# Splitting the second-to-last store of a streaming cross-entropy kernel by rows

## The chip, the cores and the metric

One NeuronCore of one Trainium2 chip runs the kernel. The metric is the device time of one execution in microseconds (us). A run's time is somewhat longer than the span that the profile shows, which goes from the first to the last instruction.

## The reference

Element by element, over two matrices of 8192 x 8192 float32:

```python
eps = 1e-7
pred = np.clip(pred, eps, 1 - eps)
return -(target * np.log(pred) + (1 - target) * np.log(1 - pred))
```

`target` holds only 0 and 1. So each element is -log(pred) or -log(1 - pred), and the kernel computes it as -Ln(|pred + target - 1|).

## The kernel before, in words

The matrices are taken as flat arrays of 128 x 524288 elements, cut into 40 chunks. A chunk of width w covers 128*w consecutive elements in memory, and tile row (partition) p holds the p-th run of w elements, so that a store of a chunk writes one contiguous block of memory, one run for each tile row. `plan` (line 17) lays them out: two of 5120 columns, 35 of 14336, and three at the end of 5632, 5632 and 1024. The last three have the numbers n-3, n-2 and n-1 and are called a, b and c. A tile row of chunk b is 22528 bytes, one of chunk c is 4096 bytes. `pred` and the result share one ring, `ring_p`, of three slots and a tail; `target` is cast to bf16 as it is loaded, into `ring_t`.

For each chunk, or each half of it, the steps are:

- `clip` (line 88, VectorE): max and min with eps.
- `log` (lines 94, 97, 98): VectorE adds target - 1, ScalarE takes the absolute value and then Ln, all in place.
- `back` (line 102, VectorE): times -1.
- `store`, to the output.

The order is written out by hand. Loads and most stores are issued from GpSimd (lines 72, 75, 79). The stores of a, b and c are issued from SyncE: `store` picks its queue by `k >= n - 3` (line 78) and issues one transfer of 128 rows (line 79), and `store_rows` (line 81) issues chunk c as three transfers, of rows 0-107, 108-119 and 120-127 (line 84). SyncE issues only these five transfers, in the order a, b, c, and each waits for the `back` of its chunk. After the last, at line 184, the program waits for all stores.

The end of the program is:

```python
        log(b, (1, 2))
        back(a, (1, 2))
        store(a)
        log(c)
        back(b, (0, 2))
        back(b, (1, 2))
        store(b)
        back(c)
        store_rows(c)
```

A DMA transfer is carried out by up to 16 DMA engines, which every queue of the core shares. In the trace each tile row of these stores is one packet on one DMA engine, and each engine that takes part in a transfer closes its share with a packet of 4 bytes.

Of the kernel before, what the change touches and what calls it, by code (L numbers as in the profile page):

```python
# [1 line left out]

# [4 lines left out]

EPS = 1e-7

BIG = 14 * 1024  # L10
FIRST = 5 * 1024
LAST = 5632
TAIL = 1024
SLOTS = 3


def plan(total):
    n = (total - 2 * FIRST - 2 * LAST - TAIL) // BIG
    assert n > 4 and total == 2 * FIRST + n * BIG + 2 * LAST + TAIL
    spots = [(FIRST, 0, 0), (FIRST, FIRST, FIRST)]  # L20
    spots += [(BIG, k % SLOTS * BIG, 0) for k in range(1, n + 1)]
    end = (n + 1) % SLOTS * BIG
    spots += [(LAST, end, 0), (LAST, end + LAST, LAST)]
    return spots + [(TAIL, SLOTS * BIG, BIG)]


@with_exitstack
def kernel(
    ctx: ExitStack,
    tc: tile.TileContext,  # L30
    pred: bass.AP,
    target: bass.AP,
    out: bass.AP,
):
    nc = tc.nc
    fp32 = mybir.dt.float32
    bf16 = mybir.dt.bfloat16
    Alu = mybir.AluOpType
    Act = mybir.ActivationFunctionType
    P = nc.NUM_PARTITIONS  # L40

    R, C = pred.shape
    spots = plan(R * C // P)
    n = len(spots)
    widths = [s[0] for s in spots]
    cols = [sum(widths[:k]) for k in range(n)]

    def chunk(ap, k):
        flat = ap.rearrange("r c -> (r c)")
        return flat[cols[k] * P : (cols[k] + widths[k]) * P].rearrange("(p w) -> p w", p=P)  # L50

    pool = ctx.enter_context(tc.tile_pool(name="rings", bufs=1))
    ring_p = pool.tile([P, SLOTS * BIG + TAIL], fp32, name="ring_p", tag="ring_p")
    ring_t = pool.tile([P, BIG + TAIL], bf16, name="ring_t", tag="ring_t")
    warm = pool.tile([1, 8], fp32, name="warm", tag="warm")

    def spot(k, part=(0, 1)):
        w, c, _ = spots[k]
        i, m = part
        return ring_p[:, c + i * w // m : c + (i + 1) * w // m]  # L60

    def spot_t(k, part=(0, 1)):
        w, _, c = spots[k]
        i, m = part
        return ring_t[:, c + i * w // m : c + (i + 1) * w // m]

    def load_p(k):
        if k == 0:
            for rows in (slice(0, P, 2), slice(1, P, 2)):
                nc.scalar.dma_start(out=spot(0)[rows], in_=chunk(pred, 0)[rows])  # L70
        else:
            nc.gpsimd.dma_start(out=spot(k), in_=chunk(pred, k))  # L72

    def load_t(k):
        nc.gpsimd.dma_start(out=spot_t(k), in_=chunk(target, k))  # L75

    def store(k):
        queue = nc.sync if k >= n - 3 else nc.gpsimd
        queue.dma_start(out=chunk(out, k), in_=spot(k))  # L79

    def store_rows(k):
        src, dst = spot(k), chunk(out, k)
        for first, last in ((0, 108), (108, 120), (120, 128)):
            nc.sync.dma_start(out=dst[first:last], in_=src[first:last])

    def clip(k, *part):
        p = spot(k, *part)
        nc.vector.tensor_scalar(  # L88
            out=p, in0=p, scalar1=EPS, scalar2=1 - EPS, op0=Alu.max, op1=Alu.min
        )  # L90

    def log(k, *part):
        p = spot(k, *part)
        nc.vector.scalar_tensor_tensor(  # L94
            out=p, in0=spot_t(k, *part), scalar=1.0, in1=p, op0=Alu.subtract, op1=Alu.add
        )
        nc.scalar.activation(out=p, in_=p, func=Act.Abs)  # L97
        nc.scalar.activation(out=p, in_=p, func=Act.Ln)  # L98

    def back(k, *part):  # L100
        p = spot(k, *part)
        nc.vector.tensor_scalar(out=p, in0=p, scalar1=-1.0, scalar2=None, op0=Alu.mult)  # L102

    with tc.manual_schedule():
        nc.vector.memset(warm, 1.0)  # L105
        load_t(0)
        load_p(0)
        load_t(1)
        load_p(1)
        load_p(2)  # L110
        nc.scalar.activation(out=warm, in_=warm, func=Act.Ln)  # L111
        for k in (0, 1):
            clip(k)
            log(k)
        load_t(2)
        back(0)
        store(0)
        back(1)
        store(1)
        load_p(3)  # L120
        a, b, c = range(n - 3, n)
        for k in range(2, n - 3):
            for h in (0, 1):
                clip(k, (h, 2))
                log(k, (h, 2))
            if k < n - 4:
                load_t(k + 1)
            else:
                load_t(a)
                load_t(b)  # L130
                load_p(c)
                load_t(c)
                back(k, (0, 2))
                for j in (a, b):
                    clip(j)
            if k < n - 4:
                back(k, (0, 2))
            back(k, (1, 2))
            store(k)
            if k + 2 < n - 3:  # L140
                load_p(k + 2)
            elif k + 2 == n - 3:
                load_p(a)
                load_p(b)
        log(a, (0, 2))
        log(a, (1, 2))
        clip(c)
        log(b, (0, 2))
        back(a, (0, 2))
# [3 lines that stand above are left out]
        log(c)  # L153
        back(b, (0, 2))
        back(b, (1, 2))
        store(b)
        back(c)
        store_rows(c)


# [1 line left out]
_INS = ['pred', 'target']  # L162
_OUTS = [((8192, 8192), 'float32')]


# [23 lines left out]
```

## Time and profile before

| | |
|---|---|
| time, median of 3 runs | 1865.05 us (1864.38 to 1865.44) |
| span of the profiled execution | 1863.3 us (the page gives no time of its own beside it) |
| VectorE busy | 1121.6 us, 60% |
| ScalarE busy | 902.4 us, 48% |
| GpSimd busy | 178.7 us, 10% |
| read from and written to memory | 536.87 MB and 268.44 MB, 432 GB/s over the span |
| SyncE's queue (q1) | 448 packets, 6.29 MB, 0.8% of the 16 DMA engines' span |
| stores a and b | 2816 KB each, 14.6 us from issue to landing (median) |
| store c | 432, 48 and 32 KB |

The median lies 1.75 us above the span of the profiled execution. The busy shares of engines are over the whole span; the change touches only the end of it, so the stretches of the last microseconds say more than the shares. In the stretches, "DMA share" is the mean busy share of the 16 DMA engines, so that 0.06 is about one engine.

### The profile page before, as it was taken

Reading aid. Unit: us, or ns where it says so; the run is one execution under the profiler, and the core shown is the slowest. Engines: PE = TensorE matmul, PEld = TensorE weight load, DVE = VectorE, ACT = ScalarE, POOL = GpSimd, SP = SyncE. Lnnn points to the kernel's source line nnn. Section 1 sums busy time; section 2 is a strip of 40 time slices with the busy share of each in tenths; the row PEclk is TensorE's granted clock in tenths of the full one; section 3 lists DMA queues with packets and bytes.
Section 4 is the critical chain, followed back from the end, with each engine's and each line's share of the span. In section 5 each row is a group of like instructions: output and inputs, shape, how many; then the busy total and the mean of one; then the engine's idle time right before and its main releaser. Section 6 shows DMA issues by size and latency. Waiting matters only on the chain.

```text
span 1863.3 us, 713 instructions
## 1 busy us (share of the span) xinstructions
DVE 1121.6 (60%) x230; ACT 902.4 (48%) x156; POOL 178.7 (10%) x120
## 2 busy tenths in 40 slices
DVE  4666555555666566655555666566655555666565
ACT  4454444455555544444445555544444445555554
POOL 1111101111110011101111110011101111110020
DMA  9999999999999999999999999999999999999999
GB/s 344 348 370 356 355 356 355 355 355 355 357 375 374 374 372 355 355 355 355 355 355 355 359 374 374 375 375 361 355 355 356 356 356 355 356 367 374 374 353 352
DMA packets 17318, 671.15 MB, mean 360 GB/s; under 512 B 1952, under 2 KB 1952, under 8 KB 2336
## 3 DMA queue, kind: packets, MB, share of 16 engines
q0 software_dynamic: 16704, 662.18, 99.0%
q1 hardware_dynamic: 448, 6.29, 0.8%
q10 hardware_dynamic: 160, 2.62, 0.4%
q14 instruction: 6, 0.05, 0.0%
HBM read 536.87 MB, written 268.44 MB: 432 GB/s over the span
## 4 chain that ended last, share of the span: by engine, by line
DMA 60%; issue 35%; ACT 3%; DVE 1%; POOL 0%; POOLq 0%; DVEq 0%; PEldq 0%
DMA ring_t<-in_target_dram 58%; DMA ring_p<-in_pred_dram 2%; ACT ring_p L98 1%; ACT ring_p L97 1%; DVE ring_p L94 1%; DVE ring_p L102 0%; POOL out_dram L79 0%; DVE ring_p L88 0%; POOL ring_t L75 0%; POOLq L75 0%; POOL ring_p L72 0%; POOLq L79 0%; DVEq L94 0%; PEldq L184 0%
## 5 line engine op out<-in xcount | busy, mean ns | idle before, releaser
L97 ACT ACTIVATE ring_p<-ring_p 128x7168 f32<-128x7168 f32 (+3 forms) x77 | 452.0, 5870 | 940.7 <-DVE ring_p L94 940.7
L94 DVE SCALAR_TENSOR_TENSOR ring_p<-ring_t,ring_p 128x7168 f32<-128x7168 bf16 (+3 forms) x77 | 558.2, 7251 | 372.0 <-DMA ring_t<-in_target_dram 370.7
L102 DVE TENSOR_SCALAR ring_p<-ring_p 128x7168 f32<-128x7168 f32 (+3 forms) x77 | 285.4, 3707 | 329.4 <-ACT ring_p L98 329.4
L98 ACT ACTIVATE ring_p<-ring_p 128x7168 f32<-128x7168 f32 (+3 forms) x77 | 452.6, 5877 | 2.4
L88 DVE TENSOR_SCALAR ring_p<-ring_p 128x7168 f32<-128x7168 f32 (+3 forms) x75 | 284.6, 3794 | 24.4 <-DMA ring_p<-in_pred_dram 24.4
L79 POOL DMA_DIRECT2D out_dram<-ring_p x37 | 128.0, 3459 | 584.4 <-DVE ring_p L102 584.2
L75 POOL DMA_DIRECT2D ring_t<-in_target_dram x40 | 29.0, 724 | 1057.2 <-DVE ring_p L94 1056.4
L72 POOL DMA_DIRECT2D ring_p<-in_pred_dram x39 | 21.8, 561 | 2.5 <-issue 2.5
L111 ACT ACT_TABLE_LOAD x1 | 1.3, 1283 | 1.9 <-issue 1.9
L105 DVE MEMSET warm<- 1x8 f32 x1 | 0.1, 65 | 0.8 <-PEq L173 0.8
L111 ACT ACTIVATE warm<-warm 1x8 f32<-1x8 f32 x1 | 0.2, 208 | 0.0
L173 POOL MEMSET const-float32-0.0<- 128x1 f32 x1 | 0.1, 99 | 0.2 <-issue 0.2
L173 POOL MEMSET const-bfloat16-1.0<- 128x1 bf16 x1 | 0.1, 102 | 0.0
L173 POOL MEMSET const-uint8-127<- 128x1 uint8 x1 | 0.1, 100 | 0.0
L173 POOL MEMSET const-float32-1.0<- 128x1 f32 x1 | 0.1, 99 | 0.0
## 6 DMA issues: line engine op xcount, KB each, us to landing
ring_p<-in_pred_dram POOLq DMA_DIRECT2D x35, 7168.0 KB, 44.3
out_dram<-ring_p POOLq DMA_DIRECT2D x35, 7168.0 KB, 31.1
ring_t<-in_target_dram POOLq DMA_DIRECT2D x35, 3584.0 KB, 31.3
ring_p<-in_pred_dram POOLq DMA_DIRECT2D x2, 2816.0 KB, 37.1
out_dram<-ring_p SPq DMA_DIRECT2D x2, 2816.0 KB, 14.6
out_dram<-ring_p POOLq DMA_DIRECT2D x2, 2560.0 KB, 27.9
ring_t<-in_target_dram POOLq DMA_DIRECT2D x2, 1408.0 KB, 26.5
ring_p<-in_pred_dram ACTq DMA_DIRECT2D x2, 1280.0 KB, 10.5
```

The source lines that it names most:

```text
L72: nc.gpsimd.dma_start(out=spot(k), in_=chunk(pred, k))
L75: nc.gpsimd.dma_start(out=spot_t(k), in_=chunk(target, k))
L79: queue.dma_start(out=chunk(out, k), in_=spot(k))
L88: nc.vector.tensor_scalar(out=p, in0=p, scalar1=EPS, scalar2=1 - EPS, op0=Alu.max, op1=Alu.min)
L94: nc.vector.scalar_tensor_tensor(out=p, in0=spot_t(k, *part), scalar=1.0, in1=p, op0=Alu.subtract, op1=Alu.add)
L97: nc.scalar.activation(out=p, in_=p, func=Act.Abs)
L98: nc.scalar.activation(out=p, in_=p, func=Act.Ln)
L102: nc.vector.tensor_scalar(out=p, in0=p, scalar1=-1.0, scalar2=None, op0=Alu.mult)
L105: nc.vector.memset(warm, 1.0)
L111: nc.scalar.activation(out=warm, in_=warm, func=Act.Ln)
L173: nc = _bacc.Bacc("TRN2", target_bir_lowering=False, num_devices=1)
```

## The change

Chunk b is stored by `store_rows` in place of `store`: three transfers on SyncE, of rows 0-111, 112-123 and 124-127, in place of one of 128 rows. They read and write the same bytes. `store_rows` now takes its cuts as arguments; chunk c keeps its own (108 and 120). The queue, the wait and the place in the order remain.

```diff
-    def store_rows(k):
+    def store_rows(k, *cuts):
         src, dst = spot(k), chunk(out, k)
-        for first, last in ((0, 108), (108, 120), (120, 128)):
+        for first, last in zip((0,) + cuts, cuts + (P,)):
             nc.sync.dma_start(out=dst[first:last], in_=src[first:last])
...
         back(b, (0, 2))
         back(b, (1, 2))
-        store(b)
+        store_rows(b, 112, 124)
         back(c)
-        store_rows(c)
+        store_rows(c, 108, 120)
```

## The prediction

> **What bounds the kernel now.** I read the page first, for what is busy over the whole span; then SyncE's waits and the DMA issues, for what the last wait is; then the stretches of the last 9 us; and at the end the trace's records of single DMA packets.
>
> The page:
>
> ```profile
> span 1863.3 us, 713 instructions
> DVE 1121.6 (60%) x230; ACT 902.4 (48%) x156; POOL 178.7 (10%) x120
> DMA  9999999999999999999999999999999999999999
> q1 hardware_dynamic: 448, 6.29, 0.8%
> ```
>
> No compute engine is busy for more than 60%, and the 16 DMA engines are busy in every slice: the kernel is bound by DMA. The change moves bytes between DMA engines in the last 16 us only, so that stretch decides. q1 is SyncE's queue.
>
> SyncE's waits and the timeline of its issues:
>
> ```profile
> SPq L184 <- DMA out_dram<-ring_p: 12.4, 3, 6.6
> ...
> 1847.07 0.35 SPq L79 DMA_DIRECT2D out_dram<-ring_p  x1
> ...
> 1847.45 0.69 DVE L102 TENSOR_SCALAR ring_p<-ring_p 128x1024 f32<-128x1024 f32 x1 [0.41 <-ACT ring_p L98]
> 1848.17 1.31 SPq L84 DMA_DIRECT2D out_dram<-ring_p  x3
> ```
>
> The last arithmetic ends at 1848.14, SyncE's last issue at 1849.48, and after that the program only waits for stores (L184, three waits, 12.4 us). So about 14 us of pure store draining stand at the end, and it is the slowest DMA engine that ends the span.
>
> The stretches (columns: window, its length, busy time of DVE, ACT and POOL, clock, DMA share, GB/s):
>
> ```profile
> 1857.00:1858.00 1.00, 0.00 (x0) 0.00 (x0) 0.00 (x0) 1.00 0.92 395
> 1859.50:1860.00 0.50, 0.00 (x0) 0.00 (x0) 0.00 (x0) 1.00 0.73 299
> 1860.00:1860.50 0.50, 0.00 (x0) 0.00 (x0) 0.00 (x0) 1.00 0.33 135
> 1860.50:1861.00 0.50, 0.00 (x0) 0.00 (x0) 0.00 (x0) 1.00 0.10 41
> 1861.00:1861.50 0.50, 0.00 (x0) 0.00 (x0) 0.00 (x0) 1.00 0.12 49
> 1861.50:1862.00 0.50, 0.00 (x0) 0.00 (x0) 0.00 (x0) 1.00 0.04 16
> ```
>
> All engines work up to about 1859.5, then they run out one by one over 2.4 us. That ragged edge is all that a different split of rows can win; what it can lose is not bounded so.
>
> **Who is late.** The packet records of q1 are 448 = 384 rows (256 of 22528 bytes for stores a and b, 128 of 4096 for c) and 64 marks of 4 bytes, one for each transfer and engine. A packet starts where the one before it on its engine ended, so they can be chained into 16 engines. Eight chains end with 9 + 1 + 1 rows of c and three marks, four with 9 + 1 rows and two marks, four have no row of c. So 108 rows went as 9 on each of 12 engines, 12 rows as one on each of 12, 8 rows as one on each of 8, and 128 rows as 8 on each of 16. I call the eight 0-7, the four 8-11, the four without c 12-15. By the same pattern (as many engines up to 16 as divide the count) 112 rows are 7 on each of 16, 12 rows one on each of 0-11, 4 rows one on each of 0-3.
>
> The ends of these chains, in span time: seven of 0-7 at 1859.67 to 1860.52; the eighth, which entered store b about a microsecond behind the rest, at 1861.44; three of 8-11 at 1859.83 to 1860.30; the fourth at 1861.97; 12-15, late since the POOL store ahead, at 1860.65 to 1860.99. The fourth of 8-11 is last because of its first two rows of c: they took 0.311 and 1.385 us where 123 of 128 took 0.159. Without that it would have ended at about 1860.6. From 1861.97 it is 1.3 us to the end of the span (landing, the remaining waits, closing barrier).
>
> **The change part by part.** (1) *Bytes.* 255 of 256 rows of 22528 took 0.836 us and the next starts 0.833 after; the total is unchanged. Engines 12-15 lose one row each: 1860.65 to 1860.99 becomes 1859.82 to 1860.16. This gains nothing by itself, since two other engines end after them. Engines 4-11 keep 8 rows of b and get one more mark (0.006 us). Engines 0-3 get nine rows and two more marks: +0.845.
>
> (2) *Issues.* Two more transfers on SyncE. The issues took 0.354 to 0.483 us, so two cost 0.75 to 0.95 on SyncE. Behind them stand the three issues of c; they move from 1848.17 to about 1848.4-1848.5, since SyncE waited there for the last L102 anyhow, and end near 1849.9. The first packet of c starts on its engine at 1857.95 because b is queued in front: over 7 us of cover, so the cost is zero. Without that cover it would be about 0.4. The 112 rows are issued at the same time as before, and nothing starts later: b's first row runs no earlier than 1851.3, when a's eight rows are through on the first engine. No compute engine waits on these stores.
>
> (3) *The closing waits.* Two more completions are waited for. Waits already fulfilled are 0.05 to 0.07 us apart, and b's come ahead of c's, so they pass while c still drains: 0 to 0.1 us, taken as zero.
>
> (4) *What the other split does to the rate of a row.* In the 128-row form every row ran at 0.836, with 16 engines at once. The trace has no 22528-byte row in any other split. The nearest is c: nearly all of its rows ran at 0.159 although the late engines were still in b, but three lost time (0.15, 1.23 and 0.58 us). From below the cost is nil (a row cannot go faster than its engine); from above it is in the rival. I take 0.2 us, nearer to c's common row than to its stalls, as a stall counts only on the engine that ends last.
>
> The sum, on the span: if the late eighth engine is one of 4-7, the end is 1861.45 without a stall like the one seen (-0.5) and 1861.97 with it (0); if it is one of 0-3, it is 1861.44 + 0.845 = 1862.28 (+0.3). The two halves even out near zero (+0.3 and about -0.3); with the 0.2 of part 4 that is +0.2. The page gives no time of the profiled execution but its span, 1863.3; the median of the runs, 1865.05, lies 1.75 above, which I carry over: 1863.3 + 0.2 + 1.75 = 1865.2.
>
> **The rivals.** *Crowding, slower.* The 12-row piece gives engines 0-11 neighbouring rows of the tile, and the 4-row piece gives 0-3 the last four. If four neighbouring rows can be read only at one engine's rate, each of these rows takes 4 x 0.836 = 3.34 us. Engines 0-3 do so twice: 6.69 in place of 0.84, +5.85, and their ends of 1859.67 to 1860.52 go to 1865.5 to 1866.4, which is 3.6 to 4.4 beyond 1861.97: 1868.6 to 1869.5. It decides once sharing adds more than 0.6 to 1.5 us in all to an engine of 0-3 (1861.97 less 1860.52 or 1859.67, less 0.845); below that the other engines cover it. For it: c's row at 0.311, twice 0.156, and the one at 1.385, both while other engines were in b. Against it: c's own 12 and 8 rows are such pieces, and four engines ran there in one 0.4 us stretch, each packet 0.159, while engines 12-15 kept 0.836 on every row. But c's rows are short, and engines were spread by their starts. A milder form (two engines meeting for part of a row) gives +1 to +3: 1866 to 1868.
>
> [...]
>
> *The split is not as said.* If 4 rows go to a single engine, it has 12 rows of b, +3.3 us on an engine that ended by 1860.52: at most 1863.9, so 1866.2 to 1867.0. Against it: 8 and 12 rows did spread over 8 and 12 engines.
>
> *The edge closes.* The stall does not recur and the late engine is among 4-11: 1864.5. The most that any split could win is the mean of the 16 ends, 1860.4: 1863.5. So faster by over 0.2% (3.7 us, about what a measurement of this kernel can tell from no change) has no room in this edge.
>
> **How the numbers follow.** The balance as summed, with or without the stall: 0.68, of it 0.15 for the edge that closes (1864.5). Crowding in full 0.12, in its milder form 0.14, another split 0.04; 0.02 for something the trace does not show. The forecast alone spans 1864.3 to 1866.3. The range reaches through the milder crowding to the lower end of the full one, 1864.2 to 1868.6, and leaves out most of the full one and a little below. Slower by over 0.2% is above 1868.8: most of the full crowding and what is unknown, 0.13. Faster 0.02, the rest 0.85.
>
> **What would show it.** Right: q1 with 464 records (384 rows and 64 - 16 + 32 = 80 marks), nearly all rows of b at 0.836, engines 12-15 finished before 1860.3, the last DMA share ending between 1861.3 and 1862.5, and three issues at 1847.1 to 1848.4 ahead of c's. Wrong: rows of 22528 at 1.6 to 3.4 us in the pieces of 12 and 4, and a DMA share of 0.2 to 0.3 that lasts beyond 1863 (crowding); or a single engine at work for 3 us (split).

## The result, and the profile after

The change makes the kernel slower: 1870.36 us (median of 7 runs, 1869.55 to 1870.70) against 1864.44 us (7 runs, 1864.25 to 1865.44) on the same chip. The ratio is 1.0030, with a 95% interval of 1.0019 to 1.0040. The forecast was 1865.2, its range ended at 1868.6, and slower by over 0.2% had a chance of 0.13. The profiled run took 1870.42 us with a span of 1868.6, so that 1.8 us lie around the span, as before.

The page of the kernel after:

```profile
span 1868.6 us, 715 instructions
DVE 1121.6 (60%) x230; ACT 902.4 (48%) x156; POOL 178.6 (10%) x120
q1 hardware_dynamic: 464, 6.29, 0.9%
```

SyncE's waits (total, times, longest):

```profile
SPq L184 <- DMA out_dram<-ring_p: 16.9, 1, 16.9
```

Arithmetic and bytes are what they were, and the 464 packets are those that were foreseen. The program waits longer for its stores. SyncE's issues, and the stretches in which the stores drain (columns as in the prediction):

```profile
1847.04 3.33 SPq L84 DMA_DIRECT2D out_dram<-ring_p  x6
```

```profile
1857.00:1858.00 1.00, 0.00 (x0) 0.00 (x0) 0.00 (x0) 1.00 1.18 338
1859.50:1860.00 0.50, 0.00 (x0) 0.00 (x0) 0.00 (x0) 1.00 0.31 107
1860.00:1860.50 0.50, 0.00 (x0) 0.00 (x0) 0.00 (x0) 1.00 0.56 164
1861.50:1862.00 0.50, 0.00 (x0) 0.00 (x0) 0.00 (x0) 1.00 1.00 242
1863.00:1864.00 1.00, 0.00 (x0) 0.00 (x0) 0.00 (x0) 1.00 0.16 66
1865.00:1866.00 1.00, 0.00 (x0) 0.00 (x0) 0.00 (x0) 1.00 0.10 41
1866.00:1867.00 1.00, 0.00 (x0) 0.00 (x0) 0.00 (x0) 1.00 0.05 20
```

The sign to read is the last two columns together. Before, from 1857 to 1858, a share of 0.92 moved 395 GB/s; after, 1.18 moves 338 (the share above 1 suggests that a packet is counted in the slice where it starts). Engines are occupied and move less: their packets take longer. One or two engines (0.05 to 0.10 of 16) are still at work until 1867.

The packet records say which packets. Before, none of the 256 rows of 22528 bytes took over 0.9 us. After, 33 did, up to 3.6 us, and together they took 34.2 us more than 0.836 each. The chain that ends last belongs to an engine with nine rows: its row of the piece of 12 took 2.58 us, its row of the piece of 4 took 3.60. Its last packet ends at 1866.93, where the last packet before ended at 1861.97: 4.96 us.

Its seven rows of the piece of 112 are less certain. Two rows begin 1 ns apart, near 1858.18, so that the packets can be linked in two ways: in one, a row of 1.17 and a row of 2.33 are among the seven, in the other all seven took 0.836. The second fits better. By it the chain is that of the engine that enters b late, at 1853.18, about a microsecond behind the other engines of 0-11. This late engine is one of 0-7 in the kernel before, and also in the runs below with 108 rows and with even and odd rows; by the first way it would be one of 8-11 here, as far as its later packets can be linked.

The rest of the 5.37 us between the two spans (1868.64 and 1863.27) comes behind the last packet: 1.71 us against 1.31.

### The profile page after: what moved, and what is told of

Same layout as the page of the kernel before. It is cut to its first block, busy times and chain, and to the rows that moved or that the text cites. A ratio compares the mean times of both kernels' runs of the same rounds, so it can differ in the third digit from the quotient of the medians.

```text
span 1868.6 us, 715 instructions
## 1 busy us (share of the span) xinstructions
DVE 1121.6 (60%) x230; ACT 902.4 (48%) x156; POOL 178.6 (10%) x120
## 4 chain that ended last, share of the span: by engine, by line
DMA 60%; issue 35%; ACT 3%; DVE 1%; POOL 0%; POOLq 0%; DVEq 0%; PEldq 0%
DMA ring_t<-in_target_dram 58%; DMA ring_p<-in_pred_dram 2%; ACT ring_p L98 1%; ACT ring_p L97 1%; DVE ring_p L94 1%; DVE ring_p L102 0%; POOL out_dram L79 0%; DVE ring_p L88 0%; POOL ring_t L75 0%; POOLq L75 0%; POOL ring_p L72 0%; POOLq L79 0%; DVEq L94 0%; PEldq L184 0%
```

## The experiments

Theory: several rows of the tile lie on one path to the DMA engines, which carries about one engine's rate (22528 bytes in 0.836 us); a transfer of 128 rows gives each engine a path of its own (before, 255 of 256 rows took 0.836 us), and the pieces do not (after, 33 took over 0.9). The path is an inference of mine: the records show how long a row takes, not what it waits for. Rivals: the number of transfers, the unequal shares (nine rows on engines 0-3), crowding where the rows are written. Times are medians, to be compared with the kernel before on the same chip, 1864.7 to 1864.9 us; ratios are to it. "Slow rows" are rows of 22528 bytes over 0.9 us in stores a and b, and "excess" is what all rows of 22528 bytes took beyond 0.836 us, summed.

**More transfers, no split by rows.**

```diff
-        store_rows(b, 112, 124)
+        for first, last in ((0, 4928), (4928, 5456), (5456, 5632)):
+            nc.sync.dma_start(out=chunk(out, b)[:, first:last], in_=spot(b)[:, first:last])
```

> Chunk b goes out in three transfers as in the changed kernel, but all of 128 rows and cut by columns (4928, 528 and 176 of 5632), so every DMA engine keeps 8 rows of each. Crowding theory (neighbouring rows are slow to read at once): no slow rows, the store drains as before, span 1863.3 plus at most 0.4 us for the added closing waits, time 1864.5 to 1865.8. Rival, more transfers are what costs: span near the changed kernel's 1868.6.

Measured: 1865.19, ratio 1.0002 (0.9992 to 1.0011). The last packet ends at 1861.93. No row of 22528 bytes was slow, and the rows of b's first piece, 19712 bytes, all took 0.733 us. The span is 1863.7, 0.4 more than before with the same end of the stores: the closing waits. So three transfers in place of one cost nothing that these runs resolve, and the rival of the number falls.

**The small pieces read from other tile rows.**

```diff
-        store_rows(b, 112, 124)
+        src, dst = spot(b), chunk(out, b)
+        nc.sync.dma_start(out=dst[0:112], in_=src[0:112])
+        nc.sync.dma_start(out=dst[112:124], in_=src[0:108:9])
+        nc.sync.dma_start(out=dst[124:128], in_=src[0:128:36])
```

> As the changed kernel, and to the same places in memory, but the pieces of 12 and 4 rows read other tile rows: 0, 9, ... 99 and 0, 36, 72, 108 in place of 112-123 and 124-127. So the last 16 rows of chunk b in the output hold other rows' values. Crowding on the tile's side: the 16 rows of the pieces take 0.84 us in place of 2 to 3.6, the last packet ends near 1862.3, span about 1864, time about 1865.8. If the crowding is where the rows are written (neighbouring memory), or comes from engines 0-3 having nine rows: unchanged, time 1870.4. If the 112-row piece has its own crowding, in between, 1867 to 1869.

Measured: 1867.88, ratio 1.0017 (1.0008 to 1.0026); last packet 1864.02, 23 slow rows with an excess of 19.9 us. Transfers, shares and places written are those of the changed kernel, only the rows read differ, and the loss against the kernel before is 3.0 us in place of 5.9: the other 2.9 us come from which rows the two small pieces read, that is, from crowding on the tile's side. But the 3.0 us that remain are more than the first line of the expectation: the last case of it, that the 112 rows crowd by themselves.

**The 112 rows alone.**

```diff
-        store_rows(b, 112, 124)
+        nc.sync.dma_start(out=chunk(out, b)[0:112], in_=spot(b)[0:112])
```

> Chunk b's piece of 112 rows alone; its last 16 rows are not stored. If only the small pieces crowd: all 112 rows at 0.836 us, span at most 1863.3, time about 1864.5 or less. If 112 rows as 7 for each engine crowd by themselves: rows of 1.2 to 2.3 us, last packet 1863 to 1865, time 1866 to 1868 though 16 rows fewer are moved.

Measured: 1867.44, ratio 1.0014 (1.0005 to 1.0023), though 16 rows fewer are moved. 22 slow rows, up to 4.0 us, excess 18.9 us, nearly that of the spread pieces (19.9). So the piece of 112 rows costs by itself 2.5 us, about as much as the two small ones. The two costs do not add up along one engine: with the spread pieces the last packet belongs to an engine of 12-15, which has rows of the 112 only, and in the changed kernel to one with nine rows.

**The cost by itself.**

```diff
-        store_rows(b, 112, 124)
+        src, dst = spot(b), chunk(out, b)
+        sets = (slice(124, 128), slice(0, 128, 32), slice(0, 128, 36))
+        for k in range(18):
+            nc.sync.dma_start(out=dst[4 * k : 4 * k + 4], in_=src[sets[k // 6]])
```

> The cost by itself: in place of chunk b's store, 18 transfers of 4 rows each, one row on each of DMA engines 0-3: six times rows 124-127, six times rows 0, 32, 64, 96, six times rows 0, 36, 72, 108. Chunk b's output is not the reference's. If four neighbours share one path of one engine's rate, and rows 32 apart share it too, a row takes 4 x 0.836 = 3.34 us in the first six, 1.67 in the next (two pairs) and 0.84 in the last. If neighbours do not share: 0.84 throughout. If only direct neighbours share and rows 32 apart do not: 3.34, 0.84, 0.84.

Stretches of this kernel; in the first the neighbours run, in the second the rows 32 apart, in the third the rows 36 apart:

```profile
1858.00:1862.00 4.00, 0.00 (x0) 0.00 (x0) 0.00 (x0) 1.00 0.22 23
1876.00:1880.00 4.00, 0.00 (x0) 0.00 (x0) 0.00 (x0) 1.00 0.25 51
1882.00:1884.00 2.00, 0.00 (x0) 0.00 (x0) 0.00 (x0) 1.00 0.25 101
```

Four engines (a share of a quarter) move 23, 51 and 101 GB/s, depending only on which four rows they read; what they write is four neighbouring runs of memory in all three. The packet records have 3.49, 1.76 and 0.836 us for a row. Four neighbours together move at about one engine's rate (four rows in 3.49 us, 0.873 each), as if they shared one path. Rows 32 apart move at half rate (1.76 us), as if they shared in pairs; which two this run does not show. This is the disputed cost, shown by itself. Its one run took 1894.0 us, which is not to be compared, since it stores 72 rows in 18 transfers in a row.

**Halves, and even and odd rows.** The same number of transfers, of rows in each (64) and of rows for each engine (4 + 4):

```diff
-        store_rows(b, 112, 124)
+        store_rows(b, 64)
```

> Chunk b as rows 0-63 and 64-127: 4 + 4 rows on every DMA engine, as many as with 128, no small piece. [...] Rival, that small pieces or unequal shares are what costs: as before, 1865.2.

```diff
-        store_rows(b, 112, 124)
+        for rows in (slice(0, 128, 2), slice(1, 128, 2)):
+            nc.sync.dma_start(out=chunk(out, b)[rows], in_=spot(b)[rows])
```

> [...] If the rows are dealt out path by path: every row 0.84, time 1865.2.

Measured: halves 1872.12, ratio 1.0039 (1.0024 to 1.0053), 86 slow rows, excess 80.5 us; even and odd 1864.89, ratio 1.0001 (0.9991 to 1.0010), one slow row. The same stretches of the halves, and then of even and odd:

```profile
1854.00:1860.00 6.00, 0.00 (x0) 0.00 (x0) 0.00 (x0) 1.00 0.96 256
1860.00:1864.00 4.00, 0.00 (x0) 0.00 (x0) 0.00 (x0) 1.00 0.97 188
```

```profile
1854.00:1860.00 6.00, 0.00 (x0) 0.00 (x0) 0.00 (x0) 1.00 0.95 399
1860.00:1864.00 4.00, 0.00 (x0) 0.00 (x0) 0.00 (x0) 1.00 0.08 33
```

At the same share, 256 against 399 GB/s. Halves cost 7.4 us, where the rival had no cost. An estimate from the run with 18 small transfers gives as much: eight rows at 1.76 us, the time of rows 32 apart, in place of 0.836 are 7.4 us more. Which rows of a half meet is not shown, and on the mean of the 16 engines the excess is 5.0 us. Even and odd rows are free: all but one of b's and a's rows took at most 0.9 us, and the expectation of 1865.2 holds.

**Fewer engines, and equal shares.**

```diff
-        store_rows(b, 112, 124)
+        nc.sync.dma_start(out=chunk(out, b)[0:108], in_=spot(b)[0:108])
```

> Chunk b's rows 0-107 alone, 9 on each of 12 DMA engines; its last 20 rows are not stored. To compare with the 112 rows alone (1867.44 us). [...] Rival, that any split other than 128 rows is slow: rows of 1.2 to 4 us as with 112, and with nine rows for each engine a time above 1867.4.

```diff
-        store_rows(b, 112, 124)
+        store_rows(b, 112)
```

> Chunk b as rows 0-111 and 112-127: 7 + 1 rows on every DMA engine, equal shares, so no engine has nine. Shared paths: the 112 rows cost what they cost alone (about 2.5 us) and 16 neighbouring rows lie on four paths, 3.5 us for each row in place of 0.84: time 1868 to 1870.5. If the ninth row on engines 0-3 and the piece of four are the main cost: 1865.5 to 1867.5.

Measured: 108 rows alone 1868.10, ratio 1.0020 (1.0010 to 1.0029); 7 + 1 rows 1868.88, ratio 1.0022 (1.0013 to 1.0031). The time of the 108 rows is one that the rival allowed (above 1867.4). I had put it lower, by an estimate of which rows meet that no run shows. The rows are not as the rival said, though: 6 over 1.2 us, the longest 1.60, excess 6.0 us in all, a third of the 112 rows' 18.9. But 2.1 us of it fell on the chain that ends last (five rows of 1.08 to 1.60), which with its ninth row would have ended near 1862.3 and ended at 1864.45. Little crowding is enough where it meets the late engine. With 7 + 1, all shares are equal, yet the excess is 32.9 us, nearly that of 112, 12 and 4 (34.2), and 4.1 of the 5.9 us are lost: unequal shares are not the main cost.

**The same shares without neighbours.**

```diff
-        store_rows(b, 112, 124)
+        src, dst = spot(b), chunk(out, b)
+        for rows in (slice(0, 128, 2), slice(1, 128, 4), slice(3, 67, 4), slice(67, 115, 4), slice(115, 128, 4)):
+            nc.sync.dma_start(out=dst[rows], in_=src[rows])
```

> The changed kernel's shares without its neighbours: chunk b's even rows (4 on every DMA engine), rows 1, 5, ... 125 (2 on every), rows 3, 7, ... 63 (1 on every), rows 67, 71, ... 111 (one on each of 12), rows 115, 119, 123, 127 (one on each of 4): again 7, 8 and 9 rows on engines 12-15, 4-11 and 0-3, in five transfers. If the crowding of rows on shared paths was the whole cost: few slow rows (the pieces of 16 and 12 rows still put two rows on some paths, 1.7 us), last packet at 1861.5 to 1863, time 1864.5 to 1866.5. If the unequal shares or the number of pieces cost: 1867 or more. If engines 12-15 had been what ends the kernel before: a gain, 1864 or less.

Measured: 1866.95, ratio 1.0011 (1.0002 to 1.0020), above the 1866.5 expected and just below the 1867 that unequal shares or the number of pieces were given. Of the 64 even rows one was slow, and 14 of the others; the excess is 16.1 us, half of the changed kernel's. The last packet is at 1864.02, on an engine with seven rows: two of its rows took 2.04 and 2.75. The late engine, with nine, ended 0.01 us earlier by the linked packets: 1.5 us of that are two slow rows, and without them its ninth row would still have put it near 1862.5, half a microsecond beyond 1861.97. Picking rows apart gives back 3.8 of the 5.9 us (2.1 remain) with the shares kept. Nothing beat the kernel before, and relieving engines 12-15 brought no gain in any run.

## Why the prediction was wrong

**Held.** The bound (the last DMA engine to drain), the engines that take part in a piece and the 464 packets, the issues that cost nothing (the six end at 1850.37, when no row of b has started), and that engines 12-15 were not what ended the kernel, though by the linked packets three of the four ended after the 1860.3 foreseen, the last near 1862.9.

**The step that failed is part 4 of the sum**, "What the other split does to the rate of a row": 0.2 us were taken, 4.5 were lost. They are what the two single rows of the engine that ends last took beyond 0.836: 1.74 and 2.77. By the linking that fits better this is the late eighth engine, and it is one of 0-3, the second half of my sum, which put its end at 1862.28. With the 4.5, and 0.17 for entering b later than before, that makes 1866.96; measured are 1866.93. (By the other linking the last engine lost 1.83 us more, in the piece of 112, and was not the late one. The step that failed is the same.)

I weighed c's rows of 0.159 as evidence that neighbours do not share. They were probably too short and too spread for it: in the kernel before, the engines reach c up to 1.8 us apart, and a row of c is over in 0.16. In the run with 18 small transfers most engines come to c within 0.5 us, and there 38 of c's 128 rows took over 0.2 us. The stalls of 0.311 and 1.385 that I set aside were probably the sign, though no run shows what caused them.

**The rival was right in mechanism and partly in price.** It gave 3.34 us for a row read with its three neighbours; the run with 18 small transfers has 3.49. For the last engine it gave 6.69 us for its two single rows; they took 2.58 + 3.60 = 6.18. The upper end of its range, 1869.5, lay below the 1870.36 measured because it added its 5.85 us to the seven engines that ended by 1860.52 and not to the late eighth: 1861.44 + 5.85 is 1867.29, 5.3 beyond 1861.97, or 1870.4 in time. That this meets the measured time is in part luck: the rows took 0.5 us less than the rival said, the closing waits and the later entry 0.6 us more than nothing. It also left out that the piece of 112 crowds by itself, which the run with 112 rows alone shows (22 slow rows, excess 18.9 us).

**Part 3 was mis-sized too**: 0 to 0.1 us for the closing waits, 0.40 measured. The last transfer's completion is the first of eight that SyncE checks, and the other seven follow 0.06 us apart after it; before, only one check came after the last landing. In the run by columns the same 0.4 shows with no other loss. With the measured terms in place (4.5 for the 0.2 of part 4, 0.3 for the ninth row on the late engine, 0.17 for its later entry, 0.4 here) the forecast's sum comes to 1870.4.

**Open.** Which tile rows an engine gets in a transfer of 112 or 108 rows is not in the trace. So it is not shown which pairs of engines met, only that they met on the tile's side in the small pieces, that 112 rows alone slow down (excess 18.9 us), and that 108 do so less (6.0).

## What to carry to other kernels

In these runs a store's cost depended on which tile rows a transfer covers, not on bytes and engines alone: a balanced transfer of 128 rows cut by columns, or into even and odd rows, cost nothing more (ratios 1.0002 and 1.0001); cut into two blocks of 64 neighbouring rows, it cost 7.4 us, with 86 slow rows. Read DMA share together with GB/s: here the same share moved 399 GB/s with even and odd rows (0.95) and 256 with halves (0.96), whose rows took longer. When you price a rival, put its cost on every engine that it can meet, the latest one first. And test a suspected shared resource with long packets started together, since short ones that arrived apart did not show it here (before, 123 of c's 128 rows took 0.159 us).

## What the runs showed of the hardware that I had not expected

A row took 3.49 us when it was read with its three neighbours, 1.76 with rows 32 apart and 0.836 with rows 36 apart: nearly in the proportion of four, two and one. Two transfers of 64 rows cost 7.4 us as halves and nothing as even and odd rows. And one row took 4.0 us in the run with 112 rows alone, more than the 3.49 of four neighbours.
